# A decoder trunk on one core: four edits to the order of work and to where weight lows are made

## The chip, the cores and the metric

The kernel runs on one core of a Trainium2 chip. The metric is the device time of one execution in microseconds (us); lower is better. A core has five engines that run side by side, each through its own instructions in order: TensorE (PE in the profile) multiplies matrices, VectorE (DVE) and ScalarE (ACT) work on tiles element by element, GpSimd (POOL) does some of the same and issues DMAs, and SyncE (SP) issues DMAs. An engine waits where an instruction needs what another engine or a transfer has not yet delivered.

## The reference

One sequence of 512 tokens with 1024 features goes through two layers. Every sub-layer normalises its input by its root mean square, and adds its output back.

```python
h = h + diff_attention(rmsnorm(h, attn_norm), ...)   # layer 0: 8 heads, two softmax maps each
h = h + sqrelu_mlp(rmsnorm(h, mlp_norm[0]), w1, w2)  # square(relu(h @ w1)) @ w2, 4096 wide
h = h + mlstm_mixer(rmsnorm(h, mlstm_norm), ...)     # layer 1: 4 heads, matrix memory
h = h + sqrelu_mlp(rmsnorm(h, mlp_norm[1]), w1, w2)
return rmsnorm(h, final_norm)
```

In the differential attention each head makes two softmax maps and subtracts the second, times a number lambda:

```python
lam = exp(sum(lq1 * lk1)) - exp(sum(lq2 * lk2)) + lambda_init
attn = p[:, 0] - lam * p[:, 1]
```

The mLSTM mixer projects its input to queries and keys (which go through a short convolution and a sigmoid), to values, to output gates and to eight gate columns; a head's scores are weighted by gate sums, multiplied by the values, normalised and gated. All arithmetic is in float32.

## The kernel before, in words

**Operands in two parts.** Each float32 matrix is split into a high part (rounded to the matmul's input type by an ACT copy) and a low part (what is missing). A product of two such matrices is three matmuls: high by high, high by low, low by high. For activations the function `operand` (L515) makes the pair: an ACT copy, and a DVE operation at L519 for the low.

**Weights.** The weights come in units of 128 x 1024 elements (512 KB), in the order of `PLAN`. `issue` (L327) loads a unit into a `raw` tile by a DMA on SP, makes `whi` with an ACT copy and `wlo` with a DVE subtraction (`split`, L532 to L534). For the units of the mLSTM's query and key columns (L349) the low is made otherwise: ACT first copies the raw weights into `whi` (L351), and then copies them with a factor of -1 into `wlo` (L352, which rounds in the same way); a DMA issued by POOL then reads the weights from memory once more and adds them to `wlo` (L353). DVE has no part in it.

There are three tiles each of `raw`, `whi` and `wlo` outside the MLPs (`ring`, L286). A unit's tiles come free when its last matmul is done. `unit` (L396) takes the next unit and issues two units ahead. For a pair of value units, `vpair_mm` (L432) takes both at once, does the eight steps of each of four token blocks with the first unit in the steps 0 to 3 and the second in the steps 4 to 7, and issues the unit after the next one only in the fourth block, when the first unit's tiles are done with (L458 to L460).

**Steps and due times.** PE's instructions run in the order in which the program names them. `tick` counts steps of work (three matmuls of 512 columns, or six of 256), and `after(n, f)` puts the function f into the program n steps later. So all the smaller work is woven in between the matmuls by numbers: `T_RS` (24) is the step at which the sums of squares of attention's input get their two matmuls (`token_scale` L562, `sums` L536), `T_RSC` (39) that of the transposes that bring the result into columns, and `D_ATT` and `D_MLS` hold the steps of each head. The other engines' instructions are put in order by the framework, for each engine, before the kernel runs; an instruction can stand ahead of ones that the program names earlier.

**Attention's start.** `group_mm` (L410) multiplies the queries and keys of the heads 0 and 1 into the four banks `mm` in 32 steps. Meanwhile DVE makes the operands' lows (L519), POOL adds up the squares (L530), and the functions `bias_table`, `bias_rows` and `constants` prepare the position bias and lambda. `constants` (L670) is due at step 31 (`T_CONST`): it takes three of the four `tmp` tiles, loads the four lambda rows into the first by a DMA on POOL (L672), multiplies and sums them on DVE (L673, L680), takes an exponential on ACT and finishes on DVE (L686 to L688). `head` (L705) scales the queries and keys of one head out of the banks (L709, L710) and splits them; `head(0)` and `head(1)` stand ahead of the first pair of value units, `values_of(0, "sc")`, which puts its products into two of the three banks `sc`. These are then brought out by `evict_v` (L583 to L588), and the first scores (L736, L737) use the same banks.

**The mLSTM's start.** A wide pair (values of head 0 with the gate columns, L1242) goes into one bank of the three `mm` and the three `ac`. Then eight units of query and key columns follow, each multiplied by `ntile_mm` (L422) into the next bank of `mm`; `evict_qk` (L1052) brings each out. `gates` (L1071) empties the wide pair's banks. Then come the value pairs 1, 2 and 3 (`values_of`, L1230), with four output gates (`out_gate`) between the pairs 1 and 2, none between 2 and 3, and four after 3. The heads' scores, value products and `squares` (L1176) are woven in.

Of the kernel before, what the change touches and what calls it, by code (L numbers as in the profile page):

```python
# [12 lines left out]
F32 = mybir.dt.float32  # L13
F32R = mybir.dt.float32r
AF = mybir.ActivationFunctionType
ALU = mybir.AluOpType
# [3 lines left out]
P = 128  # L20
T = 512
D = 1024
KT = D // P
# [15 lines left out]

T_RS, T_RSC, T_CONST, T_BIAS, T_ROWS = 24, 39, 31, 4, 14
T_ONE, T_TWO = 3, 12


# [108 lines left out]
PLAN, PAIRS = _plan()  # L154
# [31 lines left out]
def trunk(ctx: ExitStack, tc, xT, wgt, wgt2, cols, rows, rel, consts, outT):  # L186
# [11 lines left out]
    def nm(s):  # L198
        return f"{s}_{next(names)}"
# [22 lines left out]
    def tmp(n=T):  # L222
        return sp.tile([P, T], F32, tag="tmp", name=nm("tmp"))
# [5 lines left out]
    def asf(t):  # L229
        return t.bitcast(F32)  # L230
# [5 lines left out]
    def behind(ins, before):  # L236
        tc.add_manual_dep(
            ins.ins, before.ins.name,
            mybir.DependencyInfo(mybir.DependencyClass.NoSync, mybir.DependencyReason.DATA),
            reason="table order",  # L240
        )
# [8 lines left out]
    def act(out, x, func, **kw):  # L250
        name = {AF.Exp: LNSET, AF.Ln: LNSET, AF.Sigmoid: SGSET}.get(func)
        if name:
            tables(name)
        ins = nc.scalar.activation(out, x, func, **kw)  # L254
        if name:
            behind(ins, loaded["load"])
            loaded["uses"].append(ins)
# [7 lines left out]
    def after(n, fn):  # L265
        heapq.heappush(queue, (clock[0] + n, next(names), fn))
# [60 lines left out]
    def issue():  # L327

        i = state["next"]
        kind, u = PIECES[i]  # L330
        assert fits()
        state["next"] += 1
        if kind == "half":
            hi, lo = extra["half"]
            live.add(id(hi))
        else:
            hi, lo = room("whi", u), room("wlo", u)
        ready[i] = (hi, lo)
        if kind == "unit":
            w = WIDTHS[u]  # L340
            raw = room("raw", u)
            src = source(u)
            parts = 2 if u < 2 else 1
            for i in range(parts):
                c = slice(i * w // parts, (i + 1) * w // parts)
                nc.sync.dma_start(raw[:, c], src[:, c])
            for i in range(parts):
                c = slice(i * w // parts, (i + 1) * w // parts)
                if PLAN[u][0] == "m_in" and PLAN[u][1][0][1] < D:  # L349

                    act(hi[:, c], raw[:, c], AF.Copy)  # L351
                    act(lo[:, c], raw[:, c], AF.Copy, scale=-1.0)  # L352
                    nc.gpsimd.dma_start(lo[:, c], src[:, c], accum_op=ALU.add)  # L353
                else:
                    split(raw[:, c], hi[:, c], lo[:, c])
            free(raw)
            return
        if kind == "first":
            extra["pair"] = room("raw", u), room("raw", u)
            for i, r in enumerate(extra["pair"]):  # L360
                nc.sync.dma_start(r[:, :1024], source(u + i))
        r1, r2 = extra["pair"]
        a11, a12, a21, a22 = r1[:, :512], r1[:, 512:1024], r2[:, :512], r2[:, 512:1024]
        sums_of = extra["sums"]
        s1, s3, s2, s4 = (sums_of[:, i * 512 : (i + 1) * 512] for i in range(4))
        if kind == "first":
            split(r1[:, :1024], hi[:, :1024], lo[:, :1024])
        elif kind == "half":
            split(a22, hi, lo)
        elif kind == "sums1":  # L370
            vec.tensor_tensor(s1, a21, a22, op=ALU.add)
            vec.tensor_tensor(s3, a21, a11, op=ALU.subtract)
            split(sums_of[:, :1024], hi[:, :1024], lo[:, :1024])
        else:
            vec.tensor_tensor(s2, s1, a11, op=ALU.subtract)
            vec.tensor_tensor(s4, a12, s2, op=ALU.subtract)
            split(sums_of[:, 1024:], hi[:, :1024], lo[:, :1024])
            free(r1, r2)
# [120 lines left out]
    def row_of(c, n):  # L499
        return bass.AP(tensor=rows.tensor, offset=rows.offset + c, ap=[[0, P], [1, n]])  # L500

    def col(c):
        return colt[:, c : c + 1]
# [8 lines left out]
    lneps = const_col(math.log(EPS), "lneps")  # L512


    def operand(k, g0, acc):  # L515
        hi = xp.tile([P, T], F32R, tag="x", name=nm("xh"))
        lo = xp.tile([P, T], F32R, tag="x", name=nm("xl"))
        act(hi, h[k], AF.Copy, scale=col(g0 + k))
        vec.scalar_tensor_tensor(lo, h[k], col(g0 + k), asf(hi), op0=ALU.mult, op1=ALU.subtract)  # L519
        if acc is not None:  # L520
            square_in(k, acc)
        return lambda: (hi, lo)
# [95 lines left out]
    def attention(x, acc):  # L618
        with ExitStack() as st:
# [47 lines left out]
            klow = [[ap_.tile([P, T], F32R, name=f"kl{b}{m}") for m in range(2)] for b in range(2)]  # L667
            STEPS = (((3, 0),), ((2, 0),), ((1, 0), (0, 256)))

            def constants():  # L670
                rowt, prod = tmp(), tmp()
                nc.gpsimd.dma_start(rowt[:, :256], row_of(0, 256))  # L672
                vec.tensor_tensor(  # L673
                    prod[:, 0:128].rearrange("p (a d) -> p a d", a=2),
                    rowt[:, 0:256].rearrange("p (a b d) -> p a b d", a=2, b=2)[:, :, 0],
                    rowt[:, 0:256].rearrange("p (a b d) -> p a b d", a=2, b=2)[:, :, 1],
                    op=ALU.mult,
                )
                dots = tmp()
                vec.tensor_reduce(  # L680
                    dots[:, 0:2], prod[:, 0:128].rearrange("p (a d) -> p a d", a=2),
                    axis=mybir.AxisListType.X, op=ALU.add,
                )
                act(dots[:, 0:2], dots[:, 0:2], AF.Exp)
                vec.memset(coef, 1.0)
                vec.tensor_tensor(dots[:, 2:3], dots[:, 1:2], dots[:, 0:1], op=ALU.subtract)  # L686
                for c in (1, 3):
                    vec.tensor_scalar(coef[:, c : c + 1], dots[:, 2:3], -LAM0, None, op0=ALU.add)  # L688
                vec.tensor_scalar(subw, col(C_SUB), -0.5 * (1.0 - LAM0), None, op0=ALU.mult)
                for pair in klow:  # L690
                    for m in range(2):
                        o = slice(64 - 64 * m, 128 - 64 * m)
                        vec.tensor_scalar(pair[m][o], ones_f[o].to_broadcast([64, T]), 0.0, None, op0=ALU.mult)
                filled(pth[:, 1408:1536], 0.0)
                filled(ptl[:, 1408:1536], 0.0)
# [119 lines left out]
            def values_of(j, tag="mm"):  # L815

                def done(ps, b):
                    until(lambda: summed[0] >= 2 * j)
                    if b == 0:
                        vt.clear()  # L820
                        new.append(value_tiles(vp))
                    evict_v(ps, b, rsc[0], *new[0])

                new = []
                vpair_mm(x, 256, done, tag)
                vt[j] = new[0]
# [4 lines left out]
            after(T_RSC, lambda: rsc.append(token_cols(rs)))  # L831
            ps = group_mm(x)
            head(0, ps[0], ps[1], T_ONE)
            head(1, ps[2], ps[3], T_ONE + T_TWO)
            values_of(0, "sc")
            for hd in range(2, AH):
                psq, psk = ntile_mm(x), ntile_mm(x)
                head(hd, psq, psk)
                if hd % 2 == 1 and hd < AH - 1:
                    values_of(hd // 2)  # L840
# [168 lines left out]
    def mlstm(x, acc):  # L1009
        with ExitStack() as st:  # L1010
# [108 lines left out]
            def head(hd):  # L1119
# [56 lines left out]
                def squares():  # L1176
                    num0, num1, den = acc3
                    summed[0] += 1
                    pf = bank("sc")
                    mm(pf, sel[:, hs], gs[:, 1280:1792], start=True, stop=True)  # L1180
                    dd, d2, s0, s1 = scale_tile("rs2"), tmp(), chain("sq"), tmp()
                    of = [sg.tile([P, T], F32, tag="of", name=nm("of"), bufs=2) for _ in range(2)]
                    act(of[0], num0, AF.Copy)
                    vec.tensor_copy(of[1], num1)
                    act(s0, of[0], AF.Square)
                    act(s1, of[1], AF.Square)
                    pool.tensor_tensor(s0, s0, s1, op=ALU.add)
                    act(dd, pf, AF.Exp, scale=-2.0, bias=lneps)
                    act(d2, den, AF.Square, scale=math.sqrt(EPS))
                    vec.tensor_tensor(dd, dd, d2, op=ALU.max)  # L1190
                    after(D_MLS[hd][2], lambda: normed(s0, dd, of))
# [48 lines left out]

            after(T_MRS, lambda: token_scale(acc, rs))
            psv = vpair_mm(x, 264)  # L1242
            after(T_GATES, lambda: gates(psv))
            after(T_GROWS, gate_rows)
            after(T_GCOLS, gate_cols)
# [174 lines left out]
```

## Time and profile before

| | |
|---|---|
| median of 3 runs | 1174.47 us (1174.42 to 1178.26) |
| the profiled execution | 1175.75 us, of which the span of its instructions is 1174.0 us |
| DVE busy | 899.4 us, 77% of the span |
| ACT busy | 616.4 us, 53% |
| POOL busy | 191.7 us, 16% |
| data moved by DMA | 128.12 MB, 109 GB/s on average |

The profile is one execution. Times in it are counted from the first instruction. Matmuls overlap: one of 512 columns lasts 0.39 us in the rows, but the next starts about 0.23 us after it, so what PE loses is read from the starts of successive matmuls and from the idle time that a row names in brackets, with what ended it. "PEclk" is the share of PE's full clock that was granted.

### The profile page before, as it was taken

To read this page: it belongs to the slowest core of one execution; us is meant where nothing else is said; L and a number is where in the kernel's file an instruction comes from. 1 tells how busy PE (TensorE), PEld (TensorE's weight loads), DVE (VectorE), ACT (ScalarE), POOL (GpSimd) and SP (SyncE) were. 2 spreads that over 40 slices of the span, in tenths; PEclk is the share of its full clock that TensorE was granted. 3 is DMA by queue.
4 is the path that set the end of the run, shared out by engine and by line. 5 is a ranking of instruction groups with operands and counts; after the bars stand their busy time and mean duration, and the time that the engine had idled before them with its cause. 6 is when DMAs were issued, how large, how long until landed. Compare 5 with 4: busy or idle time off the path is not lost.

```text
span 1174.0 us, 17210 instructions
## 1 busy us (share of the span) xinstructions
PE 1143.0 (97%) x6718; PEld 1006.1 (86%) x6718; DVE 899.4 (77%) x1371; ACT 616.4 (53%) x926; POOL 191.7 (16%) x186
## 2 busy tenths in 40 slices
PE   8899999999999999999999999999999999999996
PEld 5778888888898998998997789888889889889895
DVE  7789888587977866967968867766698687687786
ACT  6567777564534434434557547665454353353453
POOL 5432332040000000000132212233000000000001
PEclk9899999999999999999999999999999999999998
DMA  6622222143164264362366221123325525526412
GB/s 203 203 64 75 78 73 78 65 123 123 61 168 138 64 180 134 84 169 90 92 155 147 68 90 55 54 80 104 122 82 135 161 73 139 173 66 153 135 37 72
DMA packets 37745, 128.12 MB, mean 109 GB/s; under 512 B 4479, under 2 KB 6546, under 8 KB 37664
## 3 DMA queue, kind: packets, MB, share of 16 engines
q1 hardware_dynamic: 30288, 103.38, 27.6%
q0 software_dynamic: 6256, 22.07, 9.8%
q10 hardware_dynamic: 1120, 1.57, 0.4%
q8 instruction: 53, 0.87, 0.3%
q14 instruction: 28, 0.23, 0.1%
HBM read 112.30 MB, written 4.74 MB: 100 GB/s over the span
## 4 chain that ended last, share of the span: by engine, by line
PE 81%; DVE 11%; ACT 4%; DMA 2%; issue 2%; POOL 0%; DVEq 0%; SPq 0%; ACTq 0%; POOLq 0%
PE bank L407 15%; PE bank L408 15%; PE bank L406 15%; PE bank L929 8%; PE bank L930 8%; PE bank L928 8%; DVE tmp_tmp L1058 2%; PE bank L439 1%; PE bank L438 1%; PE bank L440 1%; DVE wlo L534 1%; DMA raw<-wgt 1%; ACT whi L254 1%; PE bank L736 1%; DVE kl L720 1%
## 5 line engine op out<-in xcount | busy, mean ns | idle before, releaser
L406 PE MATMUL bank<-x_xh,whi 128*128 128x512 f32 x640 | 254.1, 397 | 4.0 <-DVE vl_v L588 2.5
L407 PE MATMUL bank<-x_xl,whi 128*128 128x512 f32 x640 | 254.9, 398 | 0.6 <-DVE x_xl L519 0.6
L408 PE MATMUL bank<-x_xh,wlo 128*128 128x512 f32 x640 | 255.4, 399 | 0.0
L254 ACT ACTIVATE whi<-raw 128x1024 fp32r<-128x1024 f32 (+2 forms) x128 | 133.4, 1042 | 115.6 <-PE bank L929 43.3
L534 DVE TENSOR_TENSOR wlo<-raw,whi 128x1024 fp32r<-128x1024 f32 (+2 forms) x120 | 152.9, 1274 | 30.2 <-ACT whi L254 29.5
L929 PE MATMUL bank<-ul,whi 128*128 128x256 f32 x544 | 153.3, 282 | 0.1
L928 PE MATMUL bank<-uh,whi 128*128 128x256 f32 x544 | 153.3, 282 | 0.0
L930 PE MATMUL bank<-uh,wlo 128*128 128x256 f32 x544 | 153.2, 282 | 0.0
L406 PEld LDWEIGHTS bank<-x_xh,whi 128*128 128x128 f32 x640 | 122.8, 192 | 32.2 <-DVE vl_v L588 3.0
L407 PEld LDWEIGHTS bank<-x_xl,whi 128*128 128x128 f32 x640 | 121.4, 190 | 28.1 <-DVE x_xl L519 1.3
L408 PEld LDWEIGHTS bank<-x_xh,wlo 128*128 128x128 f32 x640 | 121.1, 189 | 27.1 <-DVE wlo L534 0.2
L949 POOL DMA_DIRECT2D h<-work x24 | 20.8, 865 | 511.6 <-DVE work L946 392.5
L929 PEld LDWEIGHTS bank<-ul,whi 128*128 128x128 f32 x544 | 102.7, 189 | 0.5 <-DVE ul L534 0.3
L928 PEld LDWEIGHTS bank<-uh,whi 128*128 128x128 f32 x544 | 103.0, 189 | 0.1
L930 PEld LDWEIGHTS bank<-uh,wlo 128*128 128x128 f32 x544 | 102.8, 189 | 0.0
L254 ACT ACTIVATE uh<-chains 128x1792 fp32r<-128x1792 f32 (+1 forms) x38 | 56.9, 1497 | 57.6 <-DVE chains L889 57.4
L534 DVE TENSOR_TENSOR ul<-chains,uh 128x1792 fp32r<-128x1792 f32 (+1 forms) x38 | 67.3, 1771 | 23.8 <-ACT uh L254 23.3
L882 DVE SCALAR_TENSOR_TENSOR tmp_tmp<-bank,rs_rs 128x512 f32<-128x512 f32 x64 | 44.0, 688 | 44.7 <-PE bank L408 44.5
L530 POOL TENSOR_TENSOR acc_acc<-acc_acc,tmp_tmp 128x512 f32<-128x512 f32 x31 | 50.9, 1642 | 157.5 <-ACT tmp_tmp L254 152.5
L254 ACT ACTIVATE whi<-wsums 128x1024 fp32r<-128x1024 f32 x46 | 48.7, 1059 | 48.2 <-PE bank L929 30.2
L439 PE MATMUL bank<-wlo,x_xh 128*128 128x256 f32 (+1 forms) x256 | 72.2, 282 | 1.7 <-DVE wlo L534 1.7
L438 PE MATMUL bank<-whi,x_xh 128*128 128x256 f32 (+1 forms) x256 | 72.6, 284 | 0.0
(332 smaller groups left out, 2683.2 us busy)
## 6 DMA issues: line engine op xcount, KB each, us to landing
raw<-wgt SPq DMA_DIRECT2D x156, 512.0 KB, 3.8
rawx<-wgt SPq DMA_DIRECT2D x32, 512.0 KB, 4.1
h<-work POOLq DMA_DIRECT2D x24, 512.0 KB, 5.8
wlo<-wgt POOLq DMA_DIRECT2D x8, 512.0 KB, 7.3
skew<-frd POOLq DMA_DIRECT2D x8, 320.0 KB, 6.8
bias_bias<-skew POOLq DMA_DIRECT2D x8, 256.0 KB, 3.1
outT<-h SPq DMA_DIRECT2D x6, 256.0 KB, 2.5
raw<-wgt SPq DMA_DIRECT2D x2, 528.0 KB, 3.6
```

Of the source, the lines that this page charges most:

```text
L254: ins = nc.scalar.activation(out, x, func, **kw)
L406: mm(ps, whi, x[0], start=first, stop=False)
L407: mm(ps, whi, x[1], start=False, stop=False)
L408: mm(ps, wlo, x[0], start=False, stop=last)
L438: mm(ps, xh, hi[:, c], start=k == 0, stop=False)
L439: mm(ps, xh, lo[:, c], start=False, stop=False)
L530: (eng or pool).tensor_tensor(acc, acc, s, op=ALU.add)
L534: (eng or vec).tensor_tensor(lo, src, asf(hi), op=ALU.subtract)
L882: vec.scalar_tensor_tensor(m, p, 0.0, rs, op0=ALU.max, op1=ALU.mult)
L928: mm(out[name], hi[:, n], uh[:, t], start=first, stop=False, skip_group_check=late)
L929: mm(out[name], hi[:, n], ul[:, t], start=False, stop=False, skip_group_check=late)
L930: mm(out[name], lo[:, n], uh[:, t], start=False, stop=k == 3, skip_group_check=late)
```

## The change

- **Lambda rows.** They get a tile of their own, `rowt`, with room for the products and sums; its DMA on POOL is put into the program 3 steps after the start of attention. The first multiplication on them is bound behind the last of the operands' lows on DVE (`behind`, which sets the order of two instructions of one engine without a wait on another).
- **Sums of squares.** `T_RS` goes from 24 to 27.
- **Head 1.** `head(1)` stands after the first value pair, and its due times are made 16 steps shorter, which is as many as the pair has.
- **A bank passed over.** The `mm` bank that the mLSTM's wide pair wrote is taken out of the turn for 20 steps.
- **Exponential first.** In `squares` the exponential that empties the bank `pf` stands ahead of the copies and squares.
- **DMA-made lows.** The units whose lows are made by ACT and the accumulating DMA now include the six units of the value pairs 1 to 3.

```diff
-T_RS, T_RSC, T_CONST, T_BIAS, T_ROWS = 24, 39, 31, 4, 14
+T_RS, T_RSC, T_CONST, T_BIAS, T_ROWS = 27, 39, 31, 4, 14
...
-                if PLAN[u][0] == "m_in" and PLAN[u][1][0][1] < D:
+                if PLAN[u][0] == "m_in" and PLAN[u][1][0][1] < 2 * D and w == 1024:
...
+    lows = {}
+
...
-        vec.scalar_tensor_tensor(lo, h[k], col(g0 + k), asf(hi), op0=ALU.mult, op1=ALU.subtract)
+        lows[k] = vec.scalar_tensor_tensor(lo, h[k], col(g0 + k), asf(hi), op0=ALU.mult, op1=ALU.subtract)
...
+            rowt = ap_.tile([P, 388], F32, name="rowt")
+            after(3, lambda: nc.gpsimd.dma_start(rowt[:, :256], row_of(0, 256)))
+
             def constants():
-                rowt, prod = tmp(), tmp()
-                nc.gpsimd.dma_start(rowt[:, :256], row_of(0, 256))
-                vec.tensor_tensor(
+                prod, dots = rowt[:, 256:384], rowt[:, 384:388]
+                first_dots = vec.tensor_tensor(
...
-                dots = tmp()
+                behind(first_dots, lows[KT - 1])
...
-            head(1, ps[2], ps[3], T_ONE + T_TWO)
             values_of(0, "sc")
+            head(1, ps[2], ps[3], T_ONE + T_TWO - 16)
...
+                    act(dd, pf, AF.Exp, scale=-2.0, bias=lneps)
                     act(of[0], num0, AF.Copy)
...
-                    act(dd, pf, AF.Exp, scale=-2.0, bias=lneps)
...
             psv = vpair_mm(x, 264)
+
+            kept = turn["mm"].pop()
+            after(20, lambda: turn["mm"].append(kept))
```

## The prediction

> **What bounds the kernel now.** I read the page first, for the engine that the chain of work runs on.
>
> ```profile
> span 1174.0 us, 17210 instructions
> PE 1143.0 (97%) x6718; PEld 1006.1 (86%) x6718; DVE 899.4 (77%) x1371; ACT 616.4 (53%) x926; POOL 191.7 (16%) x186
> PE 81%; DVE 11%; ACT 4%; DMA 2%; issue 2%; POOL 0%; DVEq 0%; SPq 0%; ACTq 0%; POOLq 0%
> ```
>
> PE's order is fixed and its matmuls are not changed, so the edits can only move the few places where PE stands still. The chain leaves PE for DVE in 11% of the span. The view of PE's waits names those places (total us, times, longest):
>
> ```profile
> PE bank L406 <- DVE vl_v L588: 3.3, 2, 2.5
> PE bank L736 <- DVE vl_v L588: 3.1, 2, 2.4
> PE bank L542 <- DVE sl_sl L534: 1.9, 1, 1.9
> PE bank L439 <- DVE wlo L534: 1.7, 1, 1.7
> PE bank L1145 <- ACT rs_rs L254: 1.2, 1, 1.2
> PE bank L1145 <- DVE e_e L1148: 1.0, 1, 1.0
> PE bank L1115 <- DVE ig L1105: 0.6, 1, 0.6
> ```
>
> A wait can cost more than itself. I asked for the busy times in stretches of 3.41 us that end where the granted clock changes (the pairs of columns are PE, PEld, DVE, ACT, POOL; then PEclk):
>
> ```profile
> 26.39:29.80 3.41, 1.40 (x5) 0.56 (x4) 3.41 (x5) 1.58 (x2) 0.83 (x2) 1.00 0.06 6
> 29.80:33.22 3.41, 3.05 (x7) 2.47 (x8) 2.13 (x3) 1.43 (x3) 0.82 (x2) 0.50 0.47 158
> 50.28:53.70 3.41, 0.70 (x2) 0.30 (x2) 2.95 (x7) 2.58 (x4) 0.00 (x0) 1.00 0.14 19
> 53.70:57.11 3.41, 3.20 (x11) 3.02 (x12) 3.04 (x9) 0.65 (x2) 0.00 (x0) 0.50 0.69 211
> 616.90:620.31 3.41, 0.87 (x5) 0.49 (x4) 3.05 (x10) 3.40 (x8) 1.26 (x1) 1.00 0.60 115
> 620.31:623.72 3.41, 3.41 (x10) 2.64 (x9) 3.28 (x7) 3.38 (x5) 0.00 (x0) 0.50 0.00 0
> 657.86:661.27 3.41, 1.71 (x15) 1.50 (x14) 3.38 (x4) 1.81 (x3) 1.28 (x1) 1.00 0.36 137
> 661.27:664.68 3.41, 3.41 (x31) 3.41 (x31) 3.31 (x6) 1.45 (x2) 0.00 (x0) 1.00 0.47 154
> ```
>
> A stretch with PE busy 1.40 us or less is followed by one at half clock, which does half its work: 1.7 us lost. One with 1.71 us is not. So a wait of about 2 us or more, unless it falls across two stretches, costs 1.7 us on top. [...]
>
> **Attention's start (lambda rows, T_RS, head 1).**
>
> ```profile
> 26.89 0.40 PE L408 MATMUL bank<-x_xh,wlo 128*128 128x512 f32 x1
> 30.17 0.79 PE L542 MATMUL bank<-sl_sl,ones_d 128*128 128x512 f32 x1 [1.92 <-DVE sl_sl L534]
> 29.45 0.67 DVE L534 TENSOR_TENSOR sl_sl<-acc_acc,sh_sh 128x512 fp32r<-128x512 f32 x1
> 36.81 0.29 DVE L673 TENSOR_TENSOR tmp_tmp<-tmp_tmp 128x128 f32<-128x128 f32 x1 [3.99 <-DMA tmp_tmp<-rows]
> 38.79 0.42 DVE L567 TENSOR_SCALAR rs_rs<-chains 128x512 f32<-128x512 f32 x1
> 616.55 0.40 PE L407 MATMUL bank<-x_xl,whi 128*128 128x512 f32 x1
> 616.78 0.40 PE L408 MATMUL bank<-x_xh,wlo 128*128 128x512 f32 x1
> ```
>
> The last two rows give the pace: 0.23 us from start to start. PE could have begun the sums at 27.12 and their second matmul at 27.35; it began that at 30.17, 2.8 us late. Three steps more are nine matmuls, 2.1 us, so it would want the low at 29.4 and get it at 30.12: 0.7 us of wait. The dots, now bound only behind the lows, may stand ahead of that low on DVE (two of 0.29 us and three small ones, up to 0.9 us). I take 1.1 us; gain 1.7 (1.2 to 2.1). PE is then busy about 2.3 us in that stretch, so its half clock goes: 1.7.
>
> DVE stands 3.99 us for the lambda rows, and the normaliser `rs`, for which everything after waits, is late by nearly as much: it ends at 39.2, and would at about 35.6 (I take 0.4 off for what else the chain from the sums over ACT needs). With the rows there early, the heads' splits and `evict_v` start 3.6 us sooner, and head 1's share of them no longer stands between `rs` and `evict_v`. PE gets there earlier too, by 3.4 us. The two waits of the first scores (3.1 us) lose DVE's two causes; what is late next is `evict_v` of the last block, which can only follow the last matmul, three matmuls ahead of the scores: I leave 0.5, gain 2.6 (2.0 to 3.1), and their half clock goes with a chance near 0.9, 1.5 (0 to 1.7).
>
> Against it: DVE was busy 2.95 and 3.04 of 3.41 us there, and PE now comes some 7 us earlier, so DVE, spared 4 us plus a few short gaps, is late for the next transposes: 1.2 (0 to 2). The rows' DMA goes out while the first weights load; it moves 128 KB, a quarter of a unit, of which the page's issues say 3.8 us to landing: at most 0.9, I take 0.3. On POOL its issue falls into an idle stretch; head 1's bias DMA and two lows move behind the pair there, and are needed 13 steps later. Sum for attention: 1.7 + 1.7 + 2.6 + 1.5 - 1.2 - 0.3 = **-6.0 us** (-3.5 to -8).
>
> **The bank passed over.**
>
> ```profile
> raw<-wgt SPq DMA_DIRECT2D x156, 512.0 KB, 3.8
> 619.72 0.51 PE L406 MATMUL bank<-x_xh,whi 128*128 128x512 f32 x1 [2.54 <-DVE vl_v L588]
> 622.46 1.06 ACT L254 ACTIVATE whi<-raw 128x1024 fp32r<-128x1024 f32 x1
> 624.76 0.87 POOL L353 DMA_DIRECT2D wlo<-wgt  x1 [4.63 <-ACT wlo L254]
> 629.74 0.60 PE L1095 MATMUL bank<-ident,gi 128*4 128x128 f32 x4
> DMA to landing us min/median/max: 5.7/7.3/7.9
> L254 ACT ACTIVATE wlo<-raw x8: 1041/1042/1060, 592.8 to 640.6; 128x1024 fp32r<-128x1024 f32 x8
> 612.27 0.69 DVE L1054 TENSOR_TENSOR conv<-bank,rs_rs 128x512 f32<-128x512 f32 x1
> ```
>
> The first row backs the 3.8 us above. The third column tile waits 2.54 us for the wide pair's bank; with the other bank, empty at 612.96, it starts at 617.0, and the half clock after it goes: 4.4 us (2.7 + 1.7). But what is late next? The third and fourth tiles take 24 matmuls each (5.6 us) and the L1095 transposes 0.8, so the fifth wants its low at 617.0 + 11.2 + 0.8 + 0.4 = 629.4. That low is the DMA issued at 624.76; at up to 7.9 us it lands at 632.6. It hangs on the copy at 622.46, which stood on ACT behind work on the wide pair and not on PE. So a wait of 3.2 us, with a half clock of about 1.2 on average, takes the place of the 4.4: **0** (to -4.4 if ACT's order lets that copy go once its tiles are free, at 617).
>
> **Exponential first.** PE waits 1.2 us for it once (L1145, above), and a copy and a square no longer stand ahead of it on ACT. It still can't start before the `pf` matmul has ended, which is a matmul or two before PE wants the bank: **-0.7** (0 to -1.2).
>
> **DMA-made lows of the value pairs.** Six DVE operations go (1.2 to 2.3 us each) and six ACT copies of 1.04 come. The question is the time from a free tile to a landed low: two copies, 2.1 us, and 7.3 us from issue: 9.5 us, where ACT and DVE took 2.3.
>
> ```profile
> L534 DVE TENSOR_TENSOR wlo<-raw,whi x20: 1207/1224/2328, 655.2 to 793.2; 128x1024 fp32r<-128x1024 f32 x20
> 655.73 1.05 ACT L254 ACTIVATE whi<-raw 128x1024 fp32r<-128x1024 f32 x1
> 660.40 0.39 PE L439 MATMUL bank<-wlo,x_xh 128*128 128x256 f32 x1 [1.70 <-DVE wlo L534]
> 706.00:723.10 17.10, 7.89 (x28) 5.35 (x29) 1.00 0.11 32
> 723.93 1.04 ACT L254 ACTIVATE whi<-raw 128x1024 fp32r<-128x1024 f32 x1
> 726.64 0.28 PE L439 MATMUL bank<-wlo,x_xh 128*128 128x256 f32 x1
> 726.90 1.26 POOL L1142 TENSOR_SCALAR_AFFINE_SELECT e_e<-e_e 128x128 f32<-128x128 f32 x1 [4.27 <-ACT e_e L254]
> ```
>
> Pair 3, second unit: its tiles come free only when pair 2's fourth block has done its first four steps. The 28th of pair 2's 32 low matmuls (L439) starts by 723.1, and so ACT's copy goes at 723.93. PE wants the low at 726.64, the fifth L439 of pair 3. ACT and DVE just make it. By DMA: 723.93 + 2.1 + 0.1 + 7.3 = 733.4, 6.8 us late; with the shortest landing 5.2. (Tiles free at 723.4 and copies at once would make that 4.7.) I take 6.4, and 1.7 of half clock: **+8.1** (+5 to +11).
>
> Pair 1, second unit: wanted at 658.6 (660.40 less its wait), and its tiles are free one column tile and its transposes earlier, and 13 matmuls of 0.12, near 650.5. ACT's copy goes at 655.73, behind a sigmoid that waits for a late DVE. DVE gets the transposed gates 4.4 us earlier and, I take it, is 3.5 ahead: 652.2 + 2.1 + 0.1 + 7.3 = 661.7 against 657.7 (0.9 sooner, L1115's wait of 0.6 with its matmul gone): 4.0 us (2.0 if promptly copied, 7.4 as now), plus 1.4 of half clock, less the waits that go with DVE's load, 1.7 + 0.6 + 1.0: **+2.1**. Pair 2's units are issued one gate tile or more ahead: **+0.4** for the copies on ACT.
>
> The sum: -6.0 + 0 - 0.7 + 8.1 + 2.1 + 0.4 = +3.9 us, on the profiled 1175.75 us (span 1174.0 and 1.75 around it), 1179.7; the median of the runs is 1.28 lower, so 1178.4, in round numbers **1178**.
>
> **The rivals.** *Faster: the lows come in time.* If ACT's copies go as soon as tiles are free and transfers land in 5.7 us, the bank keeps its 4.4, pair 1 costs nothing and its old waits of 3.3 go, and pair 3 costs 4.7 and a half clock, 6.4. -6.0 - 4.4 - 0.7 - 3.3 + 6.4 + 0.4 = -7.6: 1167. For it: the shortest landing; against it: half took 7.3 or more. [...]
>
> *Slower: the lows queue behind in-order work.* On ACT pair 1's copy stays at 655.73 behind the sigmoid (+3.4 over my sum), and on POOL the issue of pair 3's low lands behind the scores' select, which waits for ACT too (it ran at 726.90 for 1.26): 2.1 us later. +9.4: 1184. It passes the bound once the two together land 2 us later than I took. For it: the row at 655.73; against it: DVE is relieved.
>
> *The rows stay:* the framework orders the engines as before and the gains and losses are small: 1174.
>
> **How the numbers follow.** About 0.5%, 5.9 us, is what a measurement can tell from no change: below 1168.6 is faster, above 1180.3 slower. My case 0.46 (its own spread, 1173 to 1183, puts 0.08 over the bound), the slower rival 0.26, the faster 0.24 (0.02 of it within), no effect 0.04. So faster 0.22, same 0.44, slower 0.34. The range reaches to the faster rival's time and a little past the slower one's: 1166 to 1187.
>
> **What would show it.** Right: no `DMA tmp_tmp<-rows` on DVE; no half clock near 30 and 54; PE waiting for `DMA wlo<-wgt` at the fifth column tile, and for 4 us or more at the second unit of pairs 1 and 3. Wrong: pairs 1 and 3 with waits under 2 us, or attention's start less than 3 us shorter.

## The result and the profile after

| | before | after |
|---|---|---|
| median | 1174.68 us (4 runs) | 1185.84 us (4 runs) |
| lowest to highest | 1174.42 to 1178.26 us | 1183.14 to 1185.86 us |
| the profiled execution | 1175.75 us, span 1174.0 | 1185.83 us, span 1183.8 |

The ratio after to before is 1.0073 (95% interval 1.0058 to 1.0087): the change makes the kernel 0.7% slower, 11.2 us by the medians. The forecast was 1178, with a range of 1166 to 1187.

The page of the kernel after, its head and the chain that ended last:

```profile
span 1183.8 us, 17220 instructions
PE 1144.1 (97%) x6718; PEld 1008.1 (85%) x6718; DVE 890.2 (75%) x1365; ACT 622.0 (53%) x932; POOL 192.4 (16%) x192
PE 80%; DVE 8%; ACT 5%; DMA 3%; issue 2%; POOL 1%; DVEq 0%; SPq 0%; ACTq 0%; POOLq 0%
wlo<-wgt POOLq DMA_DIRECT2D x14, 512.0 KB, 7.5
```

Six DVE operations are gone (1371 to 1365) and six ACT copies have come (926 to 932), as the change says; the accumulating transfers went from 8 to 14. The chain leaves PE for DVE in 8% of the span instead of 11, and for transfers in 3% instead of 2. Which transfers, PE's waits after show (total us, times, longest):

```profile
PE bank L439 <- DMA wlo<-wgt: 12.0, 2, 7.5
PE bank L740 <- DVE vl_v L590: 3.1, 1, 3.1
PE bank L408 <- DMA wlo<-wgt: 2.7, 1, 2.7
PE bank L544 <- DVE sl_sl L536: 1.0, 1, 1.0
PE bank L1149 <- ACT rs_rs L254: 0.9, 1, 0.9
```

The two waits of 12.0 us together stand at the second units of the value pairs 1 and 3, and the one of 2.7 us at the fifth column tile. The bank's waits for `evict_v` at a third column tile (2.5 us before) are gone. PE's rows of after say where, and for how long:

```profile
628.97 0.51 PE L408 MATMUL bank<-x_xh,wlo 128*128 128x512 f32 x1 [2.74 <-DMA wlo<-wgt]
659.16 0.58 PE L439 MATMUL bank<-wlo,x_xh 128*128 128x256 f32 x1 [4.47 <-DMA wlo<-wgt]
733.83 0.58 PE L439 MATMUL bank<-wlo,x_xh 128*128 128x256 f32 x1 [7.53 <-DMA wlo<-wgt]
```

L438 is the first of the three matmuls of a step of a value pair. Its first rows in the pairs 1, 2 and 3 start at 653.00, 706.05 and 724.62, and its last one in pair 3 at 751.74. In the kernel before the same four stand at 657.01, 706.33, 725.12 and 741.88. So the time is compared in parts, each from the first matmul of one to the first of the next (pair 3 to its last row of L438, and the rest from there to the start of PE's last matmul):

| part (us) | before | after | difference |
|---|---|---|---|
| start to attention's output projection | 200.10 | 196.84 | -3.3 |
| to the mLSTM's wide pair | 393.09 | 392.97 | -0.1 |
| wide pair to pair 1 | 63.82 | 63.18 | -0.6 |
| pair 1 to pair 2 | 49.32 | 53.06 | +3.7 |
| pair 2 to pair 3 | 18.78 | 18.56 | -0.2 |
| pair 3 | 16.77 | 27.13 | +10.4 |
| the rest | 422.42 | 422.42 | 0.0 |

The sum of the differences, +9.9, is that of the spans (1183.8 - 1174.0 = 9.8) but for a tenth. Pair 3 alone costs more than the whole change does.

The clock says why pair 3 loses 10.4 us to a wait of 7.5. The stretches of 3.41 us of the kernel after, on the grid on which its granted clock changes (columns as in the prediction: PE, PEld, DVE, ACT, POOL busy, then PEclk):

```profile
46.56:49.97 3.41, 1.50 (x8) 0.93 (x7) 3.02 (x4) 3.04 (x5) 0.95 (x1) 1.00 0.15 61
49.97:53.38 3.41, 1.96 (x10) 1.58 (x11) 3.41 (x11) 0.50 (x2) 0.00 (x0) 1.00 0.57 171
654.13:657.54 3.41, 0.55 (x5) 0.35 (x3) 3.27 (x6) 1.09 (x2) 0.00 (x0) 1.00 0.86 181
657.54:660.96 3.42, 1.80 (x8) 1.80 (x9) 3.38 (x4) 0.98 (x2) 1.28 (x1) 0.50 0.64 163
660.96:664.37 3.41, 3.41 (x18) 3.41 (x17) 1.77 (x3) 2.17 (x3) 0.00 (x0) 0.50 0.05 18
664.37:667.78 3.41, 3.41 (x31) 3.41 (x30) 0.80 (x2) 1.32 (x3) 1.28 (x1) 1.00 0.02 5
725.81:729.22 3.41, 0.49 (x5) 0.28 (x3) 2.58 (x5) 2.25 (x5) 1.10 (x2) 1.00 0.60 169
729.22:732.64 3.42, 0.00 (x0) 0.00 (x0) 0.54 (x2) 0.00 (x0) 0.00 (x0) 0.50 0.94 240
732.64:736.05 3.41, 2.22 (x10) 2.22 (x11) 0.00 (x0) 0.00 (x0) 0.00 (x0) 0.50 0.14 52
736.05:739.46 3.41, 3.41 (x11) 2.73 (x10) 0.00 (x0) 0.00 (x0) 0.00 (x0) 0.50 0.00 0
739.46:742.88 3.42, 3.42 (x26) 3.13 (x25) 1.12 (x3) 1.86 (x5) 0.29 (x1) 1.00 0.02 5
```

At pair 3 the clock is at half from 729.22 to 739.46, three stretches. There a matmul of 512 columns starts 0.43 us after the one before it (736.34 to 736.77), at full clock 0.23. PE works again from 733.83, so 5.6 us of work go at half clock, and by the granted 0.50 an estimated 2.8 of them are lost (2.6 by the two paces): 7.5 + 2.8 = 10.3, against 10.4 in the table. At pair 1 it is at half for two stretches, 5.2 us of them with PE at work: 2.6 on top of the 4.5. The chain that made pair 3's low, from ACT's copies over POOL's issue:

```profile
722.88 0.63 ACT L254 ACTIVATE sh_sh<-e_e 128x512 fp32r<-128x512 f32 x1 [0.80 <-DVE e_e L1152]
723.42 1.04 ACT L254 ACTIVATE whi<-raw 128x1024 fp32r<-128x1024 f32 x1
724.37 1.04 ACT L254 ACTIVATE wlo<-raw 128x1024 fp32r<-128x1024 f32 x1
725.72 0.88 POOL L353 DMA_DIRECT2D wlo<-wgt  x1 [3.59 <-ACT wlo L254]
```

From ACT's start to PE's (733.83) it is 10.4 us, of which 8.1 lie behind POOL's issue. ACT's order held the copy up only a little: the last matmul on the tile (L440, started at 722.39) ended at 722.67, and the copy stood behind the step in the first row, which waited for DVE. It went 0.75 us after the tile was free, as in the kernel before.

### The profile page after: what moved, and what is told of

Its sections match the earlier page's. It is cut to its first block, busy times and chain, and to the rows that moved or that the text cites. A ratio compares the mean times of both kernels' runs of the same rounds, so it can differ in the third digit from the quotient of the medians.

```text
span 1183.8 us, 17220 instructions
## 1 busy us (share of the span) xinstructions
PE 1144.1 (97%) x6718; PEld 1008.1 (85%) x6718; DVE 890.2 (75%) x1365; ACT 622.0 (53%) x932; POOL 192.4 (16%) x192
## 4 chain that ended last, share of the span: by engine, by line
PE 80%; DVE 8%; ACT 5%; DMA 3%; issue 2%; POOL 1%; DVEq 0%; SPq 0%; ACTq 0%; POOLq 0%
PE bank L407 15%; PE bank L408 15%; PE bank L406 14%; PE bank L933 8%; PE bank L934 8%; PE bank L932 8%; DMA wlo<-wgt 2%; PE bank L439 2%; PE bank L440 2%; PE bank L438 1%; DMA raw<-wgt 1%; DVE wlo L536 1%; ACT chains L254 1%; ACT whi L254 1%; PE bank L740 1%
## 5 line engine op out<-in xcount | busy, mean ns | idle before, releaser
L536 DVE TENSOR_TENSOR wlo<-raw,whi 128x1024 fp32r<-128x1024 f32 (+2 forms) x114 | 143.1, 1255 | 31.3 <-ACT whi L254 30.6
L438 PE MATMUL bank<-whi,x_xh 128*128 128x256 f32 (+1 forms) x256 | 74.1, 289 | 0.0
```

The lines of the kernel that those rows point to most:

```text
L438: mm(ps, xh, hi[:, c], start=k == 0, stop=False)
L536: (eng or vec).tensor_tensor(lo, src, asf(hi), op=ALU.subtract)
```

## The experiments

The theory after these profiles, which the expectations call A: everything the change loses is lost at the second units of the pairs 1 and 3, because their copies can start only 3 to 6 us before PE wants the low (723.42 for 726.1 at pair 3, 648.37 for 654.7 at pair 1) and two copies and an accumulating transfer take 10; the rest of the change gains. Its rivals: that the rest of the change costs something too, which the profile hides; that what is late is a queue (ACT or POOL) and not the tile; and, for what attention did not gain, that the order of the engines or the eviction itself holds the first scores. Each ratio below is to the kernel before on the same chip; its medians there were 1177.60 to 1177.93 us, so an expectation in us stands some 3 us higher there, and the ratios decide.

**The change without the DMA-made lows of the value pairs.**

```diff
-                if PLAN[u][0] == "m_in" and PLAN[u][1][0][1] < 2 * D and w == 1024:
+                if PLAN[u][0] == "m_in" and PLAN[u][1][0][1] < D:
```

> The changed kernel with the lows of the value pairs made by DVE again, all other edits kept. Theory A (late tiles: the loss is two waits for accumulating DMAs, at the second units of pairs 1 and 3, with the half clock after them): from the start of pair 1 to the end of pair 3 the changed kernel is 13.9 us longer than before, so without it 1185.8 - 13.9 = 1171.9, give or take 2; no wait of PE for a wlo DMA in the pairs; attention's start 3.3 us shorter than before and the wide pair to pair 1 about 0.6 us shorter, so 0.2 to 0.4% faster than before. Rival C (another edit costs the time): 1180 or more.

Measured: 1169.67 us, ratio 0.9935 (0.9911 to 0.9959). The other five edits together gain 0.65%, more than the 0.2 to 0.4% expected. Pair 3 is back at 16.77 us. Pair 1 to pair 2 takes 46.70, 2.6 less than before the change, which the expectation had not counted. In the profiles the kernel is 5.0 us shorter than the kernel before, by the medians 8.3: the kernel before was some 3 us slower on this chip than on the first one, and why is open. The kernel after was not run on this chip.

**The DMA-made lows alone, in the kernel before.** The diff is the same line of the change, alone.

> The kernel before with the DMA-made lows of the value pairs and nothing else of the change. Theory A: the same two waits, 4 to 5 us at pair 1 and 7 to 8 us at pair 3, and 1174.5 + 13 to 15 = 1188 to 1190. Rival D (the waits are there only because the bank and attention edits bring PE to the pairs earlier): PE arrives later here, waits under 2 us at pair 1, 1180 or less.

Measured: 1192.36 us, 1.0123 (1.0101 to 1.0145): 1.2% slower, more than the whole change. By the ratio that is what was expected (1188 to 1190). Its waits for these lows:

```profile
PE bank L439 <- DMA wlo<-wgt: 13.7, 3, 7.6
```

Pair 3 takes 26.91 us, as in the kernel after (27.13), so the other edits neither cause its loss nor hide any of it. Two of the three waits stand in pair 1 (2.95 and 3.22 us), where one of 4 to 5 was expected.

**The second unit of pair 3 by DVE again, then those of the pairs 1 and 3.** These undo the suspected part alone.

```diff
+ ... and PLAN[u][1][0][:2] != (4, D + 768):
+ ... and PLAN[u][1][0][:2] not in ((4, D + 256), (4, D + 768)):
```

> The changed kernel, but the low of pair 3's second unit is made by DVE. Theory A: its wait of 7.5 us and the half clock after it go, 1185.8 - 10.4 = 1175.4, give or take 1.5. Rival B (the six copies on ACT and the DMA traffic slow the whole stretch, and the wait only shows where): half of that or less comes back, 1180 or more.

> The changed kernel, but the lows of the second units of pairs 1 and 3 are made by DVE; the other four stay with the DMA. Theory A: both waits go, and pair 1 is also spared DVE's work on one low: 1185.8 - 10.4 - 4.6 = 1170.8, give or take 2, no more than e1 and perhaps 1 us under it. Rival B: 1176 or more.

Measured: 1174.70 us, 0.9978 (0.9967 to 0.9990), for pair 3 alone; 1168.94 us, 0.9928 (0.9908 to 0.9948), for both. Pair 3 returns to 16.77 us in both, and pair 1 to pair 2 goes from 52.61 to 46.73 with the second. The span falls by 17.4 us from the kernel after (1183.8 to 1166.4), 10.4 of it in pair 3 and 6.3 in pair 1. PE's longest waits in the kernel with both:

```profile
PE bank L740 <- DVE vl_v L590: 3.1, 1, 3.1
PE bank L408 <- DMA wlo<-wgt: 3.1, 1, 3.1
```

No wait of the value pairs is left among them. The four lows that stay with DMA cost nothing that shows, and they gain nothing that shows either: 0.9928 here and 0.9935 with all six by DVE, with intervals that overlap. Either version is one to keep: 0.7% faster than the kernel before, and with an interval wholly below that of the kernel after. By their ratios the two runs of this section are 3 to 5 us better than expected, as the first experiment was.

**A fourth tile for `whi` and `wlo` in the mLSTM, and units issued three ahead**, all six value lows by DMA as in the kernel after. It asks whether late tiles are the cause, rather than the transfer or a queue.

```diff
-        ahead(i + n)
+        ahead(i + n + deep[0])
...
+            for tag in ("whi", "wlo"):
+                ring[tag].append(gp.tile([P, 1024], F32R, name=f"{tag}y"))
+            deep[0] = 1
```

> The changed kernel with all six value lows made by DMA, and with a fourth tile each for highs and lows in the mLSTM's projections and units issued three ahead instead of two there. Theory A (the lows are late only since their tiles come free late): no wait over 1 us for a wlo DMA in the pairs or at the fifth column tile, from pair 1 to the end of pair 3 81 to 83 us instead of 98.8, and 1185.8 - 14 to 18 = 1168 to 1172. Rival B (the accumulating transfers themselves or the copies on ACT are too slow for the stretch): waits of 2 us or more stay, 1176 or more.

Measured: 1171.98 us, 0.9955 (0.9939 to 0.9972).

```profile
PE bank L1141 <- ACT e_e L254: 2.7, 1, 2.7
PE bank L410 <- DMA wlo<-wgt: 1.2, 1, 1.2
```

Of the waits for accumulating transfers 1.2 us are left, at the second column tile, and none in the value pairs. From pair 1 to the end of pair 3 it takes 51.71 + 18.55 + 16.78 = 87.0 us, against 98.75 after and 82.0 with the second units split by DVE. So tiles that come free one unit earlier, with the copies issued earlier for it, take away 11.7 of the 16.7 us with the same transfers: the late start was the cause, and not the transfer. How much of a late start was the tile and how much ACT's order this run doesn't part; the rows of pair 1 further down do. It was not free. A new wait of 2.7 us for ACT comes up at the first scores of the mLSTM, with a half clock behind it (PE busy 0.95 us from 667.45 to 670.86, PEclk 0.50 from there to 674.27), and the pairs took 4 to 6 us more than expected.

**The bank passed over, alone, in the kernel before.**

```diff
+            kept = turn["mm"].pop()
+            after(20, lambda: turn["mm"].append(kept))
```

> The kernel before with the bank passed over and nothing else. Theory A2 (the wait for the bank is replaced by one for the fifth column tile's DMA-made low): from the wide pair to pair 1 63 to 64 us as before (63.8), with a wait of about 3 us for a wlo DMA in the place of the 2.5 for the bank; what it gains comes later, from pair 1 to pair 2, where DVE is ahead and the 1.9 us for pair 1's low go (46.7 us in the changed kernel without the value lows, 49.3 before). So 2 to 3.5 us less than before, ratio 0.997 to 0.998. Rival (as a sum of the removed wait and its half clock would have it): 4.4 us from the wide pair to pair 1, 59.4 us there.

Measured: 1174.74 us, 0.9973 (0.9958 to 0.9989).

```profile
PE bank L408 <- DMA wlo<-wgt: 2.4, 1, 2.4
```

The new wait is there at the fifth tile, 2.4 us, and the old one is gone. From wide pair to pair 1 it took 61.27 us instead of 63.82, less than the 63 to 64 expected: the matmuls behind the wait start 0.23 us apart (631.85 to 632.08), so no half clock followed it, where in the kernel after (63.18) one did (PEclk 0.50 from 630.24 to 633.65). In the ten profiles with this edit and the fifth tile's low by DMA the part took 60.1 to 64.8 us. What the edit gives more steadily lies later: pair 1 to pair 2 takes 47.09 us instead of 49.32, and 46.7 to 46.9 in six other runs that have the edit, with the second units' lows by DVE and the fifth tile's by DMA. That DVE is ahead there, having the gates' bank sooner, fits with this and is argued only.

**The fifth column tile's low by DVE as well**, on top of the version with both second units split. It takes away the wait that replaced the bank's.

```diff
+ ... and PLAN[u][1][0][:2] not in ((0, 256), (4, D + 256), (4, D + 768)):
```

> As e4 (changed kernel, second units of pairs 1 and 3 made by DVE), and the fifth column tile's low is made by DVE too. Theory A2: its wait of 3.05 us and the half clock go, from the wide pair to pair 1 57 to 59.5 us instead of 61.9, and DVE gives back at most 1.5 at the gate columns: 2 to 4.5 us under e4, ratio to before 0.988 to 0.991. Rival (DVE is as late as the DMA at that place): within 1 us of e4.

Measured: 1168.94 us, 0.9938 (0.9918 to 0.9958): nothing gained. The wait for the transfer is gone, but another takes its place:

```profile
PE bank L1119 <- DVE ig L1109: 1.4, 1, 1.4
```

DVE, with one 1.2 us split more, is late at the gates. That this split is what makes DVE late is argued, and what takes back the rest of the 3.1 us is not shown. The expected 2 to 4.5 us was a miss.

**Head 1 ahead of the value pair again**, on top of that one.

```diff
+            head(1, ps[2], ps[3], T_ONE + T_TWO)
             values_of(0, "sc")
-            head(1, ps[2], ps[3], T_ONE + T_TWO - 16)
```

> As e6, but head 1 stands ahead of the first value pair again, as before the change. Theory E (the wait of the first scores, 3.1 us, is set by weight copies that stand ahead of the values' eviction on ACT and DVE, and moving head 1 changes little): within 1 us of e6 and the wait 2.5 to 4 us. Rival (moving head 1 spares the eviction work of 4 to 5 us): 2 us or more over e6.

Measured: 1170.27 us, 0.9946 (0.9927 to 0.9964), not to be told apart from 0.9938. The first scores' wait for `vl_v` is 3.4 us in two waits instead of 3.1 in one. Moving head 1 in the program does next to nothing, as theory E had it.

**The lambda rows as before**, on top of the version with both second units split.

```diff
-            rowt = ap_.tile([P, 388], F32, name="rowt")
-            after(3, lambda: nc.gpsimd.dma_start(rowt[:, :256], row_of(0, 256)))
...
+                rowt, prod = tmp(), tmp()
+                nc.gpsimd.dma_start(rowt[:, :256], row_of(0, 256))
...
-                behind(first_dots, lows[KT - 1])
```

> As e4, but the lambda rows are loaded in constants again as before the change (in tmp tiles, due at step 31, not bound). Theory G (the 3.99 us for which DVE stood waiting for the rows are the main cause of what attention's start gained): the wait on DVE is back, the first scores wait 2 to 4 us longer than in e4, and the total is 2 to 4 us over e4. Rival (what attention gained is the later sums with their half clock): within 1 us of e4.

Measured: 1175.57 us, 0.9979 (0.9968 to 0.9990): beside the other edits the rows' tile is worth about 6 us (0.9979 - 0.9928 = 0.0051), where 2 to 4 were expected. DVE's rows and PE's waits of this kernel:

```profile
38.01 0.29 DVE L675 TENSOR_TENSOR tmp_tmp<-tmp_tmp 128x128 f32<-128x128 f32 x1 [6.74 <-DMA tmp_tmp<-rows]
38.53 0.68 DVE L567 TENSOR_SCALAR chains<-bank 128x512 f32<-128x512 f32 x1
42.69 0.43 DVE L569 TENSOR_SCALAR rs_rs<-chains 128x512 f32<-128x512 f32 x1
```

```profile
PE bank L738 <- DVE vl_v L590: 4.3, 1, 4.3
PE bank L577 <- DVE rs_rs L569: 4.1, 1, 4.1
```

DVE stands 6.74 us for the rows (3.99 in the kernel before), the normaliser's last step starts at 42.69 instead of 36.63 after the change, and PE waits 4.1 us for it and 4.3 for what follows. Part of that belongs to the later sums (`T_RS`): the normaliser's first step (L567, 38.53) now stands behind the multiplication that waits for the rows, where in the kernel before it ran at 31.00, ahead of it. Attention takes 203.5 us here and 200.1 in the kernel before, so without the rows' tile the later sums and the moved head look like a loss; these are single profiles.

**The first scores four steps later** (`T_ONE` 3 to 7), on top of the same version. It asks whether the wait that stayed in attention goes when PE has other work first, or only moves.

```diff
-T_ONE, T_TWO = 3, 12
+T_ONE, T_TWO = 7, 12
```

> As e4, and attention's first scores are due 4 steps later, so that 12 further matmuls (2.8 us) stand between the last value block and the first scores. Theory E (the wait of 3.1 us is for the eviction of the last block, which runs late on ACT and DVE behind weight copies, whatever PE does): the wait falls to 0.3 to 0.8 us and attention's start up to the output projection is 2 to 3 us shorter than e4's 197.4. Rival F (DVE is late by as much for the next transposes): the wait moves to L740 behind L778, which grows from 0.8 to 2.5 or more, and the total stays within 1 us of e4.

Measured: 1177.05 us, 0.9996 (0.9986 to 1.0007).

```profile
PE bank L740 <- DVE ptl L778: 6.7, 3, 4.5
PE bank L740 <- DVE chains L799: 1.5, 1, 1.5
```

The wait at the first scores falls to 0.8 us, and 8 us of others come up in the heads behind, where PE now waits for DVE's later steps. The wait moves, as the rival that the expectation calls F has it, but neither side foresaw the size: attention takes 206.3 us instead of 197.4.

**The last two blocks of attention's first pair brought out one by one**, on top of the same version.

```diff
+            if tag == "sc" and tb >= 2:
+                done(ps, tb // 2, (tb,))
-            if tb % 2:
+            elif tb % 2:
```

> As e4, and in attention's first value pair the third and the fourth block are brought out of the bank one by one as they are done, where both were brought out after the fourth. Theory E: the third block's eviction no longer stands behind the weight copies of the fourth's time; of its 3.1 us the wait loses 1 to 2, and the kernel 1 to 2 us against e4. Rival (the fourth block's eviction alone sets it): within 0.5 us of e4.

Measured: 1173.92 us, 0.9964 (0.9951 to 0.9978), slower than without it, where a gain of 1 to 2 us or none was expected. PE's row:

```profile
48.30 0.39 PE L438 MATMUL bank<-whi,x_xh 128*128 128x256 f32 x1 [4.50 <-DVE vl_v L592]
```

The blocks 3 and 4 share a bank, and the fourth's first matmul now waits for the third's eviction. The first scores wait 0.8 us instead of 3.1; 4.5 come up ahead of them.

**The next weight unit not issued in the fourth block of that pair**, on top of the same version, so that its copies would follow the eviction on ACT and DVE.

```diff
-                if tb == NB - 1 and k == KT // 2:
+                if tb == NB - 1 and k == KT // 2 and tag != "sc":
```

> As e4, but in attention's first value pair the next weight unit is not issued in the fourth block but only after the eviction, so that its copies stand behind the eviction on ACT and DVE. Theory E: the eviction of the last two blocks then takes about 2 us from the last matmul (four operations of 0.47 us), the wait of 3.1 us at the first scores falls to 0.5 to 1.5, and attention's start up to the output projection is 1.5 to 2.5 us shorter than e4's 197.4; ratio to before 0.990 to 0.992. Rival F (as in e10: DVE is late next, or the weights are): the wait moves on, and the start is 196.5 or more.

Measured: 1170.08 us, 0.9931 (0.9916 to 0.9946), no change. The order on ACT and DVE is still what it was: a weight copy at 47.43 and a split at 48.52 stand ahead of the evictions of 48.40 and 49.67, and the wait is 3.2 us. The framework's order did not follow the program's here, so this run says nothing on what that order costs.

## Why the prediction was right or wrong, step by step

**The mechanism of the value pairs held.** The waits came at the places named, for the cause named: copies that start too late for two of them and a transfer. The fourth tile shows it, and so do the two runs in which DVE makes these lows. At pair 3 the start was late because of the tile; at pair 1 about half of the wait came from ACT's order (below).

**Pair 3: +10.4 measured, +8.1 forecast (+5 to +11).** The wait was 7.5 for 6.4: the transfer took 8.1 us from issue to PE's start where 7.3 was taken, and the copies ran when it was assumed. The larger miss is the half clock: one stretch, 1.7 us, was put down, and 2.8 was lost over three. The prediction's rule, that a stretch with PE busy 1.40 us or less is followed by one at half clock, held here (0.49 us from 725.81, PEclk 0.50 from 729.22); that the one stretch is all did not.

**Pair 1: +3.7 measured, +2.1 forecast.** The wait was 4.5 for 4.0, the half clock 2.6 for 1.4, and 2.6 us of old waits went (49.32 to 46.70) where 3.3 were counted. By the run with the bank alone those went because of the bank (47.09), not because DVE makes fewer lows. The three make +4.5; of the 0.8 too much, 0.5 is a wait for `e_e` that the run with both second units split still has here and the kernel after has not.

The slower rival, copies behind in-order work, came true in part. No select stood before POOL's issue for pair 3, and ACT made pair 1's `whi` 7.4 us sooner than before, but not promptly:

```profile
646.61 0.40 PE L408 MATMUL bank<-x_xh,wlo 128*128 128x512 f32 x1
648.15 0.31 ACT L254 ACTIVATE gs<-pr 4x128 fp32r<-4x128 f32 x1 [1.55 <-DVE pr L1110]
648.37 1.04 ACT L254 ACTIVATE whi<-raw 128x1024 fp32r<-128x1024 f32 x1
649.98 0.63 ACT L254 ACTIVATE tmp_tmp<-tmp_tmp 128x512 f32<-128x512 f32 x1 [0.56 <-DVE tmp_tmp L1062]
650.51 1.04 ACT L254 ACTIVATE wlo<-raw 128x1024 fp32r<-128x1024 f32 x1
651.85 0.87 POOL L353 DMA_DIRECT2D wlo<-wgt  x1 [3.88 <-ACT wlo L254]
```

The first row is the tile's last matmul, and the raw weights, issued at 643.30 and 3.9 us on their way, landed near 647.2. The first copy stood behind a gate copy that waited 1.55 us for DVE, and the second behind a sigmoid that waited 0.56. From the first copy to POOL's issue 3.5 us passed, where 2.2 were taken. With both copies prompt the low would have landed near 656.8, an estimate from these rows, against the 654.7 at which PE wanted it: 2.1 us of wait, the prediction's own 2.0 for prompt copies, instead of 4.5.

The rival's time, 1184, is the nearest to what was measured. The range reached up to 1187 for that rival, and the sum's own spread went to 1183 only. So that the result lies in the range is in part luck.

**The bank passed over: 0 forecast, -0.6 measured** up to pair 1, by the trade foreseen: 2.5 us of the bank for 2.7 of a transfer, each with one stretch at half clock (620.31 before, 630.24 after).

**Exponential first and the copies on ACT: -0.7 and +0.4 forecast, -0.2 measured** from pair 2 to pair 3. The -0.7 is not seen. With the exponential first and no value lows by DMA the part took 18.78 us and the wait 1.2, as in the kernel before; with the value lows alone and the exponential as it was, 18.52 and 0.9. So the little that was gained goes with the value lows.

**Attention: -3.3 measured, -6.0 forecast.** Two parts are as foreseen. DVE no longer waits for the rows, and the second sums wait 1.0 us instead of 1.9 (forecast 1.1), with no half clock near 30 (PE busy 2.41 us from 29.49 to 32.90, PEclk 1.00). The step that failed is "I leave 0.5" for the first scores, which still wait 3.1 us. Two assumptions in it fell. The normaliser was ready at 37.06 instead of the 35.6 worked out. The prediction took DVE's wait for the rows off, but left the start of the normaliser's chain where it was; with the sums put later (`T_RS`), and a weight split ahead of it on DVE, it starts 1.5 us later. The first row is of the kernel before, the others are of the kernel after:

```profile
31.00 0.69 DVE L565 TENSOR_SCALAR chains<-bank 128x512 f32<-128x512 f32 x1 [0.89 <-PE bank L542]
32.47 0.68 DVE L567 TENSOR_SCALAR chains<-bank 128x512 f32<-128x512 f32 x1
35.18 0.69 DVE L560 TENSOR_TENSOR chains<-chains 128x512 f32<-128x512 f32 x1 [2.03 <-ACT chains L254]
36.63 0.43 DVE L569 TENSOR_SCALAR rs_rs<-chains 128x512 f32<-128x512 f32 x1
```

And the evictions are not the next thing on ACT and DVE. The rows of the kernel after around PE's wait:

```profile
47.28 1.06 ACT L254 ACTIVATE whi<-raw 128x1024 fp32r<-128x1024 f32 x1
48.38 1.23 DVE L536 TENSOR_TENSOR wlo<-raw,whi 128x1024 fp32r<-128x1024 f32 x1 [0.31 <-ACT whi L254]
49.52 0.48 DVE L590 SCALAR_TENSOR_TENSOR vl_v<-bank,rscol_rscol,vh_v 128x256 fp32r<-128x256 f32 x1
50.03 0.47 ACT L254 ACTIVATE vh_v<-bank,rscol_rscol 128x256 fp32r<-128x256 f32 x1 [0.38 <-DVE vl_v L590]
50.54 0.48 DVE L590 SCALAR_TENSOR_TENSOR vl_v<-bank,rscol_rscol,vh_v 128x256 fp32r<-128x256 f32 x1
51.17 0.47 PE L740 MATMUL bank<-kh_kh,q_q 128*128 128x512 f32 x1 [3.12 <-DVE vl_v L590]
```

The first eviction on DVE (49.52) stands behind a weight split of 1.23 us, which waits for a weight copy on ACT; ACT's second eviction (50.03) waits for that one, and DVE's second (50.54) for ACT's. So the last ends at 51.02, where the last matmul of the pair is done at 46.9. That this order costs the wait is argued from these rows and not shown: the run that was to change the order didn't, and the two that worked round it put the wait elsewhere. What sets the eviction's place there stays open. The half clock that went near 54 is no firm gain either. The wait of 3.1 us fell across two stretches here (1.50 and 1.96 us busy); in the version with the second units split the same wait falls into one:

```profile
48.00:51.42 3.42, 0.30 (x2) 0.29 (x2) 3.06 (x6) 2.11 (x4) 0.00 (x0) 1.00 0.18 46
51.42:54.83 3.41, 3.41 (x14) 3.23 (x14) 3.11 (x12) 1.36 (x4) 0.00 (x0) 0.50 0.74 241
```

PE is busy 0.30 us in the first of them, and the clock is at half in the second. In five other runs with this attention it took 196.5 to 198.0 us, 2.1 to 3.6 less than the kernel before, so the forecast's own sign of being wrong, less than 3 us, is neither clearly met nor clearly missed.

**The sum.** Forecast +3.9, measured +9.9 in the spans and +11.2 by the medians. The differences of the terms: attention +2.7, pair 3 +2.3, pair 1 +1.6, and about -0.6 for the bank. Two terms of one kind, the half clock behind a long wait, make 1.1 and 1.2 of it. The medians are 1.3 us further apart than the spans, since the profiled execution of the kernel before lay 1.1 us above its median and that of the kernel after did not.

## What to carry to other kernels

Before an operation is moved from an engine to a transfer, write down for each place when its buffer comes free and when its result is wanted: here the same edit was free for four units, though without a gain that shows, and cost 17 us at two. Look also at what stands ahead of the copies on their engine. The units with too little lead should keep the old way, which beat both kernels, and a further buffer is the other remedy. For a wait longer than a stretch of the clock (3.41 us in these traces), don't take one stretch at half clock for granted: here one with PE busy 2.22 us was followed by another at half, and one with 3.05 us by full clock.

## What the runs showed of the hardware

- **One stretch of work did not always end the half clock.** At full clock, stretches of 3.41 us with PE busy 1.50 us (46.56 above) and 1.71 us (657.86 in the kernel before) were followed by full clock, and those with 1.40 us (26.39 in the kernel before) and 1.27 us (626.82 after) by half. At half clock 1.80 us (657.54) and 2.22 us (732.64) were not enough: the next stretch was at half too. But not all of a stretch was needed: 3.05 and 3.20 us were followed by full clock in the kernel before (29.80 and 53.70). Where between these figures the line lies, the traces of the two kernels don't show.
- **The accumulating transfers took about twice as long as plain loads, and spread.** The 14 of the kernel after took 6.1 to 8.1 us from issue to landing, half of them 7.5 or more, and pair 3's 8.1, where plain loads of the same 512 KB had a median of 3.8.
- **The same kernel's time differs from run to run.** The kernel before took 1174.42 to 1178.26 us in four runs on the first chip, and 1174.44 to 1181.00 us in twenty on the chip of the run with the first scores four steps later. A difference of 2 us in one part of one profile is not yet a result.
